# A hybrid decoder layer whose input- and output-projection weights are split once, kept in DRAM as split halves, and reloaded by later chunks

## The chip, the cores and the metric

One core of one Trainium2 chip runs the whole layer. The metric is the device time of one execution in microseconds (us). In what follows PE is the tensor engine, DVE the vector engine, ACT the scalar engine, and SP the engine whose only work here is to issue DMAs, one after the other in the order of its program. All matmuls that matter are float32r matmuls.

## The reference, cut to what matters

```python
h = concat([meta, x])                                  # 16 + 2048 positions, 1024 channels
u = _rmsnorm(h, mix_norm_g)
p = u @ w_in                                           # 1024 x 1792
y = concat([pool_mixer(p_pool), conformer_conv(p_bval, p_bgate), rglru(p_cgate, p_cx)])
h = h + y @ w_out                                      # 1024 x 1024
u = _rmsnorm(h, mlp_norm_g)
h = h + square(relu(u @ w_up)) @ w_down                # 1024 x 4096, 4096 x 1024
out = _rmsnorm(h, final_norm_g)[16:]
```

## The kernel before

Channels lie on the 128 partitions, positions along the row. The 2048 positions are worked in four chunks, c = 0 to 3, of 512 (chunk 0 has the 16 meta positions besides). To keep float32 accuracy at the speed of float32r, every operand is split into a high and a low half: ACT writes `hi` (a copy rounded to float32r) and DVE writes `lo = src - hi` (`split`, L109 to L111), and each product is made as three matmuls, hi·hi, hi·lo, lo·hi.

**Weights.** A block of weights (128 output channels by 1024 inputs) comes as two DMAs of 128x512 float32 (256 KB) into tiles `wr` (6 buffers). Each is split into a tile `wh` of 128x2x512 (hi and lo side by side, 512 KB, 4 buffers). One `wh` tile serves 4 blocks of 128 inputs times three products, 12 matmuls, before its buffer comes free. Class `Weights` (L244) runs down a list of sources: at each item it has splits made up to 4 tiles ahead (`LA_SPLIT`) and DMAs up to 10 tiles ahead (`LA_DMA`).

**Items.** PE's work is a list of items (L923 on): W (a block of the input projection), O (a block of the output projection, 8 to a chunk), U and D (the MLP's up and down projections). The order is W of chunks 0 and 1 together, O of 0, the last four W blocks of chunk 1, then for every chunk U and D, and after D of chunk 0 the eight O items of chunk 1 and the fourteen W items of chunk 2; after D of chunk 1 likewise O of 2 and W of 3; O of 3 stands inside D of 2. "The O stage of chunk c" below means those eight items, 16 weight tiles.

**What else runs in the O stage of chunks 1 and 2.** The finished chunk's output norm is made and stored (`gen_final`, `d_out<-h`). Each O item's result is added on DVE to a piece of the input x, that a DMA brings into a tile `xr` (`evac_o`, L708; 2 `xr` buffers). The next chunk but one's x is loaded through the same two `xr` buffers, squared for its norm on ACT and split into eight `U` tiles (`gen_x`, L404); the W items that follow need all eight. An O item accumulates in a PSUM tile `pm` with 4 buffers, so item j cannot start before item j-4 has been added and its bank freed. Two short matmuls by a matrix of ones (`colsum`, L322, tile `pb`) sum the squares over the channels; a square root on ACT and a RECIPROCAL on DVE follow (`rsqrt_of`).

**Order.** The program text gives each operation a place, but the instruction order on each engine is set by a list scheduler with a model of its own, in which the weight splits have a raised priority (`tc.high_priority(EARLY)`). Every engine, SP too, then executes its list strictly in order: an instruction that waits for a semaphore holds up all behind it.

Of the kernel before, what the change touches and what calls it, by code (L numbers as in the profile page):

```python
# [25 lines left out]
F32 = mybir.dt.float32  # L26
# [4 lines left out]
P = 128  # L31
D = 1024
KB = D // P
# [11 lines left out]
WR = 6  # L45
# [20 lines left out]
for _n, _c in _VECS:  # L66
# [5 lines left out]
_WORDER = (  # L72
    [("bv", 0, 2), ("bg", 0, 4), ("bv", 1, 3), ("bg", 1, 5)]
    + [("cx", i, 10 + i) for i in range(4)]
    + [("ua", i, i) for i in range(2)]
    + [("z", i, 6 + i) for i in range(4)]
)


def build(nc, tc, x0, xr, w_in, w_out, w_fold, w_up, w_down, vecs, gates, pools, pws, out):  # L80
# [10 lines left out]
    dp = es.enter_context(tc.tile_pool(name="dp", bufs=1, space=bass.MemoryType.DRAM))  # L91
# [3 lines left out]
    def nm(s):  # L95
        uid[0] += 1
        return f"{s}_{uid[0]}"

    def t_(tag, cols, bufs, dt=F32):
        shape = [P] + (list(cols) if isinstance(cols, (list, tuple)) else [cols])  # L100
        return sb.tile(shape, dt, name=nm(tag), tag=tag, bufs=bufs)
# [7 lines left out]
    def split(hi, lo, src):  # L109
        A.activation(out=hi, in_=src, func=AF.Copy)  # L110
        V.tensor_tensor(out=lo, in0=src, in1=hi.bitcast(F32), op=ALU.subtract)  # L111
# [21 lines left out]
    cst = {}  # L133

    wo_fold = dp.tile([KB, P, 512], F32, name="wo_fold", tag="wo_fold")
    sums = [dp.tile([P, 2048], F32, name=f"sums_{u}", tag=f"sums_{u}") for u in range(NU)]

    def w_raw(src, tag="xr", bufs=2, queue=nc.sync):
        n = src.shape[-1]
        t = t_(tag, 512, bufs)[:, :n]  # L140
        queue.dma_start(out=t, in_=src)
        return t

    def split_to(hi, lo, raw, scale=None):
        if scale is None:
            split(hi, lo, raw)
        else:
            A.activation(out=hi, in_=raw, func=AF.Copy, scale=scale)
            V.scalar_tensor_tensor(out=lo, in0=raw, scalar=scale, in1=hi.bitcast(F32), op0=ALU.mult, op1=ALU.subtract)
# [6 lines left out]
    def gen_fold():  # L156

        pl, pw = b_tile(), b_tile()
        r1, r2 = w_raw(pools), w_raw(pws)
        split(pl[:, 0, :256], pl[:, 1, :256], r1)  # L160
        split(pw[:, 0, :512], pw[:, 1, :512], r2)
        yield 1300

# [78 lines left out]


    class Weights:  # L244
        def __init__(self, srcs):
            self.srcs = srcs
            self.raw = {}
            self.hl = {}
            self.nd = 0
            self.ns = 0  # L250

        def dma(self, n):
            while self.nd < min(n, len(self.srcs)):
                self.raw[self.nd] = w_raw(self.srcs[self.nd](), "wr", WR, nc.sync if self.nd > 1 else nc.scalar)
                self.nd += 1

        def split(self, n):
            while self.ns < min(n, len(self.srcs)):
                self.dma(self.ns + 1)
                t = t_("wh", (2, 512), WH, F32R)  # L260
                with tc.high_priority(EARLY):
                    split(t[:, 0], t[:, 1], self.raw.pop(self.ns))
                self.hl[self.ns] = t
                self.ns += 1

# [683 lines left out]
    def sources(it):  # L949

        kind, c, j, _ = it
        if kind == "U" and c:
            m1, m2, s = w_up[2 * j], w_up[2 * j + 1], sums[j]
            aps = (
                (m1, 0), (m1, 512), (s, 0), (s, 1536), (s, 1024), (s, 512), (m2, 512),
            )
            return ("U", j), [lambda a=a, c0=c0: a[:, c0 : c0 + 512] for a, c0 in aps]
        if kind == "W":
            a = w_in[_WORDER[j][2]]
        elif kind == "U":  # L960
            a = w_up[j]
        elif kind == "D":
            a = w_down[j // KB, j % KB]
        else:
            return ("O", j), [lambda: wo_fold[j], lambda: w_out[j]]
        return (kind, a.offset if hasattr(a, "offset") else j, j), [lambda a=a, c0=c0: a[:, c0 : c0 + 512] for c0 in (0, 512)]

    srcs, windex, last = [], [], None
    for it in items:
        key, aps = sources(it)  # L970
        if it[0] == "U":
            key = ("U", it[1] > 0, it[2])
        if it[0] == "W":
            key = ("W", _WORDER[it[2]][2])
        if key != last:
            first = len(srcs)
            srcs.extend(aps)
            last = key
        windex.append(first)
    wts = Weights(srcs)  # L980

# [7 lines left out]
    for n, it in enumerate(items):  # L989
# [29 lines left out]
        if kind == "W":  # L1019
            wk, i, _ = _WORDER[j]  # L1020
# [96 lines left out]
def _program():  # L1117
    nc = bacc.Bacc("TRN2", target_bir_lowering=False, num_devices=1, dynamic_dma_scratch_size=1024)
    args = [nc.dram_tensor("d_" + n, list(s), F32, kind="ExternalInput").ap() for n, s in _SHAPES.items()]
    out = nc.dram_tensor("d_out", [NCH, KB, P, NT], F32, kind="ExternalOutput").ap()  # L1120
    with tile.TileContext(nc) as tc:
        build(nc, tc, *args, out)
    return nc
# [8 lines left out]
```

## Time and profile before

| | |
|---|---|
| median of 3 runs | 1967.27 us (1966.43 to 1970.16) |
| the profiled execution | 1964.15 us, of which its span is 1962.2 us |
| PE busy | 1932.9 us, 99% of the span |
| DVE busy | 1508.6 us, 77% |
| ACT busy | 1097.9 us, 56% |
| DMA traffic | 285.07 MB, mean 145 GB/s |

The profile is of one execution. A row of the groups of instructions reads: line, engine, operation, the tile written and the tiles read, the count, then busy time in us and the mean duration of one in ns, and the idle time of the engine just before them with what ended it. In a timeline each row has the start in us, the duration in us, the engine, the line and the tiles; a figure in square brackets is the idle time ahead of it and what released it. "SPq" is SP's queue of DMA issues. A row of the table by stretches has the length of the stretch, the busy time of each engine with its number of instructions, the granted clock of PE as a share of the full one (PEclk), the busy share of the 16 DMA engines, and GB/s.

### The profile page before, as it was taken

The numbers are of one execution on the slowest core, as the hardware profiler recorded it, in microseconds if no ns is written. First come the engines' busy times: TensorE is split into PE (matmuls) and PEld (weight loads), VectorE is DVE, ScalarE is ACT, GpSimd is POOL, SyncE is SP. The second block draws the span as 40 slices with busy tenths as digits, with TensorE's granted clock in tenths as the row PEclk, the third lists the DMA queues.
The fourth block names the chain that finished last, engine by engine and source line by source line (L and its number), as shares of the span: only waits on it lengthen the run. The fifth ranks groups of instructions, "written<-read, shape, count | busy, mean of one in ns | idle before, by whom it ended". The sixth has DMA issues, their size and how long they took to land.

```text
span 1962.2 us, 29710 instructions
## 1 busy us (share of the span) xinstructions
PE 1932.9 (99%) x10648; PEld 1664.7 (85%) x10648; DVE 1508.6 (77%) x2419; ACT 1097.9 (56%) x1837; POOL 0.2 (0%) x4
## 2 busy tenths in 40 slices
PE   8999999999999999999999999999999999999998
PEld 8888878878888789898898778988989889889897
DVE  7986689977756899985776799986768597656477
ACT  6575463646544536675575453775658356445374
POOL 0000000000000000000000000000000000000000
PEclk9999999999999999999999999999999999999999
DMA  6412456645755435353444543544435434545354
GB/s 199 135 44 76 129 169 218 212 159 171 267 174 162 144 92 168 90 166 108 146 133 125 184 127 108 151 115 141 139 117 163 132 103 151 170 137 151 113 173 150
DMA packets 160035, 285.07 MB, mean 145 GB/s; under 512 B 17552, under 2 KB 23824, under 8 KB 159888
## 3 DMA queue, kind: packets, MB, share of 16 engines
q1 hardware_dynamic: 158304, 281.55, 46.6%
q8 instruction: 83, 1.36, 0.3%
q10 hardware_dynamic: 1584, 1.64, 0.2%
q14 instruction: 64, 0.52, 0.1%
HBM read 255.85 MB, written 27.26 MB: 144 GB/s over the span
## 4 chain that ended last, share of the span: by engine, by line
PE 77%; DVE 11%; DMA 6%; issue 3%; ACT 3%; SPq 1%; ACTq 0%; DVEq 0%
PE pm L278 47%; PE pm L302 11%; PE pw L302 9%; PE pm L292 7%; DVE wh L111 3%; DMA s<-d_w_up 2%; DMA xr<-d_xr 2%; DVE ca L535 1%; DMA t<-d_w_up 1%; DVE t L569 1%; DVE fr L821 1%; ACT wh L110 1%; DVE U L795 0%; DMA sums<-s 0%; PE pb L311 0%
## 5 line engine op out<-in xcount | busy, mean ns | idle before, releaser
L110 ACT ACTIVATE wh<-wr 128x512 fp32r<-128x512 f32 x828 | 517.1, 627 | 710.4 <-PE pm L278 482.9
L278 PE MATMUL pm<-U,wh 128*128 128x512 f32 (+1 forms) x3504 | 788.2, 384 | 0.6 <-DVE wh L111 0.6
L278 PEld LDWEIGHTS pm<-U,wh 128*128 128x128 f32 x3504 | 635.2, 188 | 141.0 <-DVE wh L111 1.0
L111 DVE TENSOR_TENSOR wh<-wr,wh 128x512 fp32r<-128x512 f32 x828 | 567.4, 689 | 208.6 <-ACT wh L110 204.1
L278 PE MATMUL pm<-H,wh 128*128 128x512 f32 (+1 forms) x2112 | 450.2, 372 | 8.0 <-ACT wh L110 6.5
L278 PEld LDWEIGHTS pm<-H,wh 128*128 128x128 f32 x2112 | 370.6, 190 | 82.9 <-ACT wh L110 6.5
L302 PE MATMUL pm<-H,wh 128*128 128x256 f32 x2304 | 292.5, 282 | 2.3 <-DVE wh L111 1.4
L302 PEld LDWEIGHTS pm<-H,wh 128*128 128x128 f32 x2304 | 282.3, 188 | 5.2 <-DVE wh L111 2.2
L302 PE MATMUL pw<-H,wh 128*128 128x256 f32 x1728 | 223.2, 282 | 1.6 <-DVE fr L821 1.6
L302 PEld LDWEIGHTS pw<-H,wh 128*128 128x128 f32 x1728 | 212.0, 189 | 4.6 <-DVE fr L821 3.9
L292 PE MATMUL pm<-U,wh 128*128 128x512 f32 (+1 forms) x768 | 176.1, 388 | 0.0
L292 PEld LDWEIGHTS pm<-U,wh 128*128 128x128 f32 x768 | 140.2, 188 | 30.9 <-DVE U L795 0.2
L535 DVE SCALAR_TENSOR_TENSOR ca<-Pbv,vec,ca 128x512 f32<-128x512 f32 x180 | 128.1, 748 | 0.0
L850 DVE TENSOR_TENSOR h<-h,pm 128x512 f32<-128x512 f32 (+1 forms) x106 | 71.6, 675 | 60.5 <-PE pm L278 45.6
L795 DVE TENSOR_TENSOR U<-fr,U 128x512 fp32r<-128x512 f32 x128 | 87.6, 687 | 11.4 <-ACT fr L794 11.4
L793 ACT ACTIVATE U<-fr 128x512 fp32r<-128x512 f32 x128 | 79.6, 624 | 1.9
L794 ACT ACTIVATE fr<-fr 128x512 f32<-128x512 f32 x128 | 79.3, 622 | 1.1
L821 DVE TENSOR_TENSOR fr<-pw,fr 128x512 f32<-128x512 f32 x96 | 66.1, 689 | 4.5 <-PE pw L302 1.9
L346 DVE TENSOR_TENSOR ss<-ss,fr 128x512 f32<-128x512 f32 (+1 forms) x82 | 53.3, 650 | 15.9 <-ACT fr L345 15.3
L337 DVE RECIPROCAL rs<-rs 128x512 f32<-128x512 f32 (+2 forms) x17 | 53.9, 3169 | 10.8 <-ACT rs L335 10.6
L535 DVE SCALAR_TENSOR_TENSOR ca<-h,vec,ca 128x512 f32<-128x512 f32 x60 | 42.8, 748 | 0.1
L841 ACT ACTIVATE fr<-fr 128x512 f32<-128x512 f32 x48 | 30.0, 625 | 12.1 <-DVE fr L840 11.8
(211 smaller groups left out, 1153.0 us busy)
## 6 DMA issues: line engine op xcount, KB each, us to landing
wr<-d_w_down SPq DMA_DIRECT2D x272, 256.0 KB, 2.9
wr<-d_w_up SPq DMA_DIRECT2D x208, 256.0 KB, 2.9
wr<-sums SPq DMA_DIRECT2D x192, 256.0 KB, 3.3
wr<-d_w_in SPq DMA_DIRECT2D x90, 256.0 KB, 2.7
xr<-d_xr SPq DMA_DIRECT2D x56, 256.0 KB, 2.8
wr<-wo_fold SPq DMA_DIRECT2D x32, 256.0 KB, 2.6
wr<-d_w_out SPq DMA_DIRECT2D x32, 256.0 KB, 2.6
s<-d_w_up SPq DMA_DIRECT2D x32, 256.0 KB, 3.8
```

Of the source, the lines that this page charges most:

```text
L110: A.activation(out=hi, in_=src, func=AF.Copy)
L111: V.tensor_tensor(out=lo, in0=src, in1=hi.bitcast(F32), op=ALU.subtract)
L278: T.matmul(ps[:, : s1 - s0], w[k // 4][:, a, (k % 4) * P : (k % 4 + 1) * P], rhs[k][:, b, s0:s1], start=(k == 0 and j == 0), stop=(k == KB ...
L292: T.matmul(ps[:, : s1 - s0], w[k // 4][:, a, (k % 4) * P : (k % 4 + 1) * P], rhs[k][:, b, s0:s1], start=(k == 0 and j == 0), stop=(k == KB ...
L302: T.matmul(ps, w[:, a, k * P : (k + 1) * P], op[k // 2][:, b, (k % 2) * 256 : (k % 2) * 256 + 256], start=(k == 0 and j == 0), stop=(k == ...
L337: V.reciprocal(rs[:, c0:c1], rs[:, c0:c1])
L535: V.scalar_tensor_tensor(out=a, in0=o.ub[i][:, k : k + NT], scalar=vc("cw", i * CONVK + k), in1=a, op0=ALU.mult, op1=ALU.add)
L793: A.activation(out=f[:, 0], in_=r, func=AF.Square)
L794: A.activation(out=r, in_=r, func=AF.Square)
L795: V.tensor_tensor(out=f[:, 1], in0=r, in1=f[:, 0].bitcast(F32), op=ALU.subtract)
L821: V.tensor_tensor(out=out.rearrange("p (a c) -> p a c", a=2), in0=ps.rearrange("p (a c) -> p a c", a=2), in1=x.unsqueeze(1).broadcast_to([ ...
L850: V.tensor_tensor(out=h, in0=h, in1=ps[:, : s1 - s0], op=ALU.add)
```

## The change

When a W or O weight tile is split for the first time, the split tile `wh` (hi and lo) is also stored to DRAM, into `w_kept` or `o_kept`. Each later use of the same block loads the 512 KB from there straight into a `wh` buffer: no `wr` tile, no ACT copy, no DVE subtraction. U and D weights are handled as before. The load is traced where the split was, at the same raised priority, and goes out on SP, as does the store.

```diff
+    w_kept = [[dp.tile([P, 2, 512], F32, name=f"wk_{b}_{q}", tag=f"wk_{b}_{q}") for q in range(2)] for b in range(14)]
+    o_kept = [[dp.tile([P, 2, 512], F32, name=f"ok_{j}_{q}", tag=f"ok_{j}_{q}") for q in range(2)] for j in range(KB)]
...
         def dma(self, n):
             while self.nd < min(n, len(self.srcs)):
-                self.raw[self.nd] = w_raw(self.srcs[self.nd](), "wr", WR, nc.sync if self.nd > 1 else nc.scalar)
+                if self.srcs[self.nd][2] is not None:
+                    self.nd += 1
+                    continue
+                self.raw[self.nd] = w_raw(self.srcs[self.nd][0](), "wr", WR, nc.sync if self.nd > 1 else nc.scalar)
                 self.nd += 1
...
                 t = t_("wh", (2, 512), WH, F32R)
+                _, keep, kept = self.srcs[self.ns]
                 with tc.high_priority(EARLY):
-                    split(t[:, 0], t[:, 1], self.raw.pop(self.ns))
+                    if kept is not None:
+                        nc.sync.dma_start(out=t.bitcast(F32), in_=kept)
+                    else:
+                        split(t[:, 0], t[:, 1], self.raw.pop(self.ns))
+                if keep is not None:
+                    nc.sync.dma_start(out=keep, in_=t.bitcast(F32))
                 self.hl[self.ns] = t
...
+        keep = (None, None)
         if kind == "W":
-            a = w_in[_WORDER[j][2]]
+            b = _WORDER[j][2]
+            if c > 1 or ("W", b) in seen:
+                return [(None, None, t) for t in w_kept[b]]
+            a, keep = w_in[b], w_kept[b]
...
         else:
-            return ("O", j), [lambda: wo_fold[j], lambda: w_out[j]]
+            if c:
+                return [(None, None, t) for t in o_kept[j]]
+            return [(lambda: wo_fold[j], o_kept[j][0], None), (lambda: w_out[j], o_kept[j][1], None)]
+        return [(lambda a=a, c0=c0: a[:, c0 : c0 + 512], keep[c0 // 512], None) for c0 in (0, 512)]
```

Of the 828 `wh` tiles 112 are now loaded whole (64 of W, 48 of O), and 44 are stored (28 and 16). Lines behind the edits move down, by 13 in the region of interest: `xr<-d_xr` of `gen_x` is L412 before and L425 after, that of `evac_o` L713 and L726, `d_out<-h` L873 and L886.

The scheduler orders SP, DVE, ACT and PE anew. Three places matter.

SP, in the O stage of chunk 1, before. The rows begin with the last store of the finished chunk's output (`d_out<-h`). The rows of L412 load the x tiles of chunk 2, from the second on; the row of L713 is the x piece for O item 2; `wr` rows are weights.

```order
L873 DMA d_out<-h_351_2160 128x512
L412 DMA xr_939_5549<-d_xr 128x512
L412 DMA xr_942_5557<-d_xr 128x512
L141 DMA wr_969_5652<-wo_fold_75 128x512
L141 DMA wr_970_5654<-d_w_out 128x512
L141 DMA wr_980_5703<-d_w_in 128x512
L412 DMA xr_945_5565<-d_xr 128x512
L141 DMA wr_981_5705<-d_w_in 128x512
L713 DMA xr_952_5607<-d_xr 128x512
L141 DMA wr_988_5745<-d_w_in 128x512
L412 DMA xr_956_5615<-d_xr 128x512
```

The same place after. `wh<-ok_6_0` is the first half of O item 6, `ok_7` belongs to item 7, `wk_2_0` to the first W item of chunk 2.

```order
L886 DMA d_out<-h_343_2228 128x512
L271 DMA wh_960_5755<-ok_6_0_116 128x1024
L425 DMA xr_919_5583<-d_xr 128x512
L425 DMA xr_922_5591<-d_xr 128x512
L271 DMA wh_961_5757<-ok_6_1_117 128x1024
L271 DMA wh_966_5791<-ok_7_0_118 128x1024
L425 DMA xr_925_5599<-d_xr 128x512
L726 DMA xr_930_5635<-d_xr 128x512
L271 DMA wh_967_5793<-ok_7_1_119 128x1024
L425 DMA xr_934_5643<-d_xr 128x512
L425 DMA xr_937_5651<-d_xr 128x512
L271 DMA wh_972_5827<-wk_2_0_80 128x1024
```

The second and third x tile now stand behind the load of item 6's first half, the fourth and the x piece of item 2 behind item 7's first half, and the fifth and sixth behind item 7's second half; before, raw weight loads stood there. Each `wh` load waits for the last matmul of the tile four places ahead of it in the list of weights, whose buffer it takes.

In the O stage of chunk 2 SP has the same pattern with single rows: the second x tile of chunk 3 stands behind item 6's first half, the third behind its second half, the fourth behind item 7's first half, the x piece of O item 2 and the fifth to eighth tile behind item 7's second half.

DVE, at the end of the O stage of chunk 2, before: the last of chunk 3's eight `U` tiles, the low half for the sum of its squares (`hl`), then the addition that ends O item 3 (`h<-pm,xr`), and two rows on the RECIPROCAL for chunk 3's norm.

```order
L149 SCALAR_TENSOR_TENSOR U_1770_10421<-xr_1771_10422,vec_1_69,U_1770_10421 128x512
L111 TENSOR_TENSOR hl_1781_10471<-ss_1741_10324,hl_1781_10471 128x512
L715 TENSOR_TENSOR h_1779_10466<-pm_1777_10439,xr_1778_10464 128x512
L111 TENSOR_TENSOR wh_1809_10609<-wr_1787_10488,wh_1809_10609 128x512
L337 RECIPROCAL rs_1783_10477<-rs_1783_10477 128x512
```

The same place after.

```order
L151 SCALAR_TENSOR_TENSOR U_1704_10317<-xr_1705_10318,vec_1_69,U_1704_10317 128x512
L111 TENSOR_TENSOR hl_1713_10361<-ss_1677_10226,hl_1713_10361 128x512
L350 RECIPROCAL rs_1715_10367<-rs_1715_10367 128x512
L728 TENSOR_TENSOR h_1711_10356<-pm_1709_10329,xr_1710_10354 128x512
L728 TENSOR_TENSOR h_1720_10401<-pm_1718_10374,xr_1719_10399 128x512
```

The RECIPROCAL has moved ahead of the addition that ends O item 3. In the O stage of chunk 1 the addition still stands ahead of the RECIPROCAL.

SP, at the start of the program, after: behind the loads of x for chunk 0 the first two rows are stores of split tiles, and only then come the next raw weights. Before, the raw weights stood directly behind the loads of x.

```order
L395 DMA t_25_166<-d_x0 128x528
L275 DMA wk_2_0_80<-wh_27_170 128x1024
L275 DMA wk_2_1_81<-wh_28_174 128x1024
L143 DMA wr_36_200<-d_w_in 128x512
L143 DMA wr_38_206<-d_w_in 128x512
```

The two stores wait for the DVE halves of the first two splits, and the raw weights wait behind them. PE's order is that of before but for the places of single `pb` matmuls.

More of the change, by code (lines that the diff above doesn't have):

```diff
@@ L956, in sources @@
             )
-            return ("U", j), [lambda a=a, c0=c0: a[:, c0 : c0 + 512] for a, c0 in aps]
+            return [(lambda a=a, c0=c0: a[:, c0 : c0 + 512], None, None) for a, c0 in aps]
+        keep = (None, None)
         if kind == "W":
-            a = w_in[_WORDER[j][2]]
+            b = _WORDER[j][2]
+            if c > 1 or ("W", b) in seen:
+                return [(None, None, t) for t in w_kept[b]]
+            a, keep = w_in[b], w_kept[b]
         elif kind == "U":
@@ L964, in sources @@
         else:
-            return ("O", j), [lambda: wo_fold[j], lambda: w_out[j]]
-        return (kind, a.offset if hasattr(a, "offset") else j, j), [lambda a=a, c0=c0: a[:, c0 : c0 + 512] for c0 in (0, 512)]
-    srcs, windex, last = [], [], None
-    for it in items:
[L970 to L974, printed above, removed]
+            if c:
+                return [(None, None, t) for t in o_kept[j]]
+            return [(lambda: wo_fold[j], o_kept[j][0], None), (lambda: w_out[j], o_kept[j][1], None)]
+        return [(lambda a=a, c0=c0: a[:, c0 : c0 + 512], keep[c0 // 512], None) for c0 in (0, 512)]
+    srcs, windex, last, seen = [], [], None, set()
+    for it in items:
+        kind, c, j, _ = it
+        key = (kind, j if kind != "W" else _WORDER[j][2])
+        if kind == "U":
+            key += (c > 0,)
         if key != last:
             first = len(srcs)
-            srcs.extend(aps)
+            srcs.extend(sources(it))
             last = key
+            seen.add(key)
         windex.append(first)
```

## Prediction

> **What bounds the kernel now.** The page's first part comes first, then PE's own waits.
>
> ```profile
> PE 1932.9 (99%) x10648; PEld 1664.7 (85%) x10648; DVE 1508.6 (77%) x2419; ACT 1097.9 (56%) x1837; POOL 0.2 (0%) x4
> PE pm L278 <- ACT wh L110: 6.5, 1, 6.5
> PE pb L327 <- ACT hl L110: 4.2, 3, 1.8
> ```
>
> PE is busy nearly throughout; its longest wait for a weight split is the single one before the first matmul. The rows of the two halves of a split and the stretches of the projections follow.
>
> ```profile
> L110 ACT ACTIVATE wh<-wr 128x512 fp32r<-128x512 f32 x828 | 517.1, 627 | 710.4 <-PE pm L278 482.9
> L111 DVE TENSOR_TENSOR wh<-wr,wh 128x512 fp32r<-128x512 f32 x828 | 567.4, 689 | 208.6 <-ACT wh L110 204.1
> 183.00:229.00 46.00, 46.00 (x200) 36.86 (x198) 24.04 (x37) 17.39 (x29) 0.00 (x0) 1.00 0.49 148
> 609.00:660.00 51.00, 47.98 (x198) 37.81 (x198) 40.76 (x55) 26.79 (x44) 0.00 (x0) 0.97 0.59 187
> 660.00:738.00 78.00, 78.00 (x336) 63.02 (x335) 75.06 (x133) 32.86 (x54) 0.00 (x0) 1.00 0.35 107
> 1088.00:1136.00 48.00, 46.68 (x198) 36.31 (x196) 39.48 (x54) 24.23 (x41) 0.00 (x0) 1.00 0.62 198
> 1136.00:1215.00 79.00, 79.00 (x339) 63.44 (x339) 76.01 (x127) 33.61 (x55) 0.00 (x0) 1.00 0.36 107
> ```
>
> The stretches are the O stage of chunk 0, then O of chunk 1, W of 2, O of 2 and W of 3. In both W stages DVE is busy 96% of the time and PE all of it: no split is late there. The only loose stretches are the O stages of chunks 1 and 2, and there PE does not wait for weights. PE's timeline at both places, and SP's:
>
> ```profile
> 608.82 3.18 PE L278 MATMUL pm<-H,wh 128*128 128x512 f32 x13
> 650.42 0.50 PE L327 MATMUL pb<-hl,ones 128*128 128x512 f32 x1 [1.83 <-ACT hl L110]
> 652.60 7.12 PE L278 MATMUL pm<-H,wh 128*128 128x512 f32 x24 [0.53 <-DVE h L715]
> 1087.90 3.18 PE L278 MATMUL pm<-H,wh 128*128 128x512 f32 x13
> 1129.59 0.50 PE L328 MATMUL pb<-hl,ones 128*128 128x512 f32 x1 [0.23 <-DVE hl L111]
> 1130.19 5.85 PE L278 MATMUL pm<-H,wh 128*128 128x512 f32 x24
> 628.32 1.00 SPq L412 DMA_DIRECT2D xr<-d_xr  x2
> 633.15 0.33 SPq L412 DMA_DIRECT2D xr<-d_xr  x1
> 635.02 0.33 SPq L713 DMA_DIRECT2D xr<-d_xr  x1
> 1105.52 1.04 SPq L412 DMA_DIRECT2D xr<-d_xr  x2
> ```
>
> O of chunk 1 begins at 608.82. Seven of its eight items run without a break, 7 × 5.6 us at the rate worked out below and two short sums, to about 648.5; the last starts at 652.60, 43.8 us in, after waits for the norm's sum and for `h L715`, the addition that frees its PSUM bank. In chunk 2 the break is from about 1128 to 1130.19, 42.3 in. What PE waits for is the chain of x loads through two `xr` buffers: from the second x tile on (628.32, 19.5 in; 1105.52, 17.6 in) each load needs a buffer that ACT and DVE have just emptied.
>
> **The change, part by part.** *Removed.* 112 splits: 112 × 0.627 = 70 us of ACT and 112 × 0.689 = 77 us of DVE. Where they go, PE does not wait for them, so I count nothing; at most the waits of the two O stages and single waits in the U stages shrink.
>
> *The loads.* The nearest rows for 512 KB are the loads and stores of 256 KB.
>
> ```profile
> wr<-d_w_out SPq DMA_DIRECT2D x32, 256.0 KB, 2.6
> xr<-d_xr SPq DMA_DIRECT2D x56, 256.0 KB, 2.8
> sums<-s SPq DMA_DIRECT2D x32, 256.0 KB, 3.9
> 1144.77 70.47 PE pm L278 x302
> 490.00:540.00 50.00, 50.00 (x217) 40.52 (x217) 38.59 (x63) 25.38 (x43) 0.00 (x0) 1.00 0.80 266
> ```
>
> A matmul takes 70.47/302 = 0.233 us of PE, a weight tile of 12 takes 2.8. A `wh` load goes out when the tile four ahead is done and has three tiles, 8.4 us, to land. It takes between 2.6 and twice that, 5.2, so it is hidden; I count nothing. Bandwidth: in W, 28 × 0.262 MB more in 78 us is 94 GB/s on top of 107. In O of chunk 0, 16 stores of 0.524 MB in 46 us are 182 on top of 148, 330 GB/s, where the row of 266 at a busy share of 0.80 makes the ceiling 333. The stores have over 8 us of slack; 0 to 4 us, I take 1.
>
> *The start.* The raw weights move behind two stores.
>
> ```profile
> 6.14 8.70 SPq L141 DMA_DIRECT2D wr<-d_w_in  x9
> 7.75 0.69 DVE L111 TENSOR_TENSOR wh<-wr,wh 128x512 fp32r<-128x512 f32 x1 [0.62 <-ACT wh L110]
> 11.38 1.20 ACT L110 ACTIVATE wh<-wr 128x512 fp32r<-128x512 f32 x2
> 23.27 6.02 PE L278 MATMUL pm<-H,wh 128*128 128x264 f32 x47
> ```
>
> The third weight goes out after 8.44 instead of at 6.14, so its split moves from 11.4 to about 14 or 15; PE gets to it in earnest at 23.27. Nothing counted, -1 to +2.
>
> *SP's list in the O stages: the term that matters.* A `wh` load now waits on SP for PE. Queued behind it are the x tiles and the x pieces of the O items, and for those wait ACT, DVE and in the end PE. Before, the raw load of a tile waited for the split six tiles ahead of it in the list, and that for PE to be done four tiles further ahead; now it waits for PE four tiles ahead. What stands behind a weight load of the same number is held about six tiles, 17 us, longer, unless the list was changed to suit.
>
> ```profile
> SPq L141 <- DVE wh L111: 1276.6, 741, 10.1
> 631.09 0.63 ACT L345 ACTIVATE fr<-xr 128x512 f32<-128x512 f32 x1 [1.29 <-DMA xr<-d_xr]
> 632.37 0.75 DVE L149 SCALAR_TENSOR_TENSOR U<-xr,vec,U 128x512 fp32r<-128x512 f32 x1
> 634.24 0.75 DVE L149 SCALAR_TENSOR_TENSOR U<-xr,vec,U 128x512 fp32r<-128x512 f32 x1
> 651.86 0.69 DVE L715 TENSOR_TENSOR h<-pm,xr 128x512 f32<-128x512 f32 x1 [0.34 <-DMA xr<-d_xr]
> 1128.84 0.69 DVE L111 TENSOR_TENSOR hl<-ss,hl 128x512 fp32r<-128x512 f32 x1
> 1130.85 3.35 DVE L337 RECIPROCAL rs<-rs 128x512 f32<-128x512 f32 x1
> ```
>
> From landing (631.09) to a free buffer (632.37 + 0.75) an x tile takes 2.0 us, the second of a pair 1.9 more; a load 2.8 from issue to landing; 0.4 is added for the `wh` load's own issue. Times from the stage's start, x tiles counted from 1:
>
> Chunk 1. Tiles 2 and 3 stand behind item 6's first half, which waits for 9 weight tiles, 25.2: tile 2 goes out at 25.6, lands 28.4, is used 30.4; tile 3 used 32.3. Tile 4 stands behind item 7's first half (11 tiles, 30.8): out 31.2, landed 34.0, used 36.0. Item 2's x piece needs tile 3's buffer: out 32.3, landed 35.1, added 35.8. Item 6 needs that bank and starts at 35.8 instead of 33.6. Tile 5: out 36.0, used 40.8; tile 6 used 42.7; tile 7: out 40.9, used 45.7. Item 3's piece takes its buffer: out 45.8, landed 48.6, added 49.3, and item 7 starts at 49.3, where before it was 43.8: **+5.5 us**.
>
> Chunk 2. Tile 2 used 30.4; tile 3 behind 10 weight tiles, out 28.4, used 33.2; tile 4 behind 11, used 36.0; item 2's piece behind 12, out 34.0, added 37.5, so item 6 starts 3.9 late. Tile 5 used 40.9, tile 6 42.8, tile 7 45.8, tile 8 out 42.9, used 47.7. Now the RECIPROCAL stands ahead of item 3's addition on DVE: `hl` done 48.4; from there to the end of the RECIPROCAL is 1134.20 - 1129.53 = 4.7 by the rows, 53.1; added 53.8, where before it was 42.3: **+11.5 us**.
>
> The landings of all DMAs into `xr`, and the stretches at the breaks of before (the third figure from the end is the clock):
>
> ```profile
> DMA to landing us min/median/max: 2.0/2.8/4.5
> 652.00:656.00 4.00, 3.47 (x10) 2.73 (x10) 3.72 (x2) 1.32 (x2) 0.00 (x0) 0.57 0.60 191
> 1127.00:1131.00 4.00, 2.70 (x10) 1.43 (x9) 3.70 (x7) 3.05 (x6) 0.00 (x0) 1.00 0.63 197
> ```
>
> Bounds: were SP to reach these rows as early as before, both terms are zero or a little below; with the five loads in series at the longest landing, 4.5 us, each is 8.5 more. I take the median, 2.8.
>
> *The clock.* After the break of about 4 us in chunk 1, with two lone matmuls in it, PE ran 4 us at 0.57 of its clock, a loss of 4 × 0.43 = 1.7 us; after the shorter one of chunk 2 it did not. Of the breaks ahead (2.2 and 7.8 in chunk 1, 3.9 and 10.7 in chunk 2) two are new and near 4 or longer: 2 × 1.7 = **+3.4**. The Trainium skill ("TensorE: Matmul & The Clock Gate", Part 1) says that PE falls to half its clock after an idle window of about 3.4 us on a free-running counter and gets it back after a busy window; the trace agrees on the two breaks above. By that rule the break of 3.9 may miss a whole window, and this term would be an estimated 1.7 instead of 3.4, the sum 1.7 less.
>
> *Sum.* 5.5 + 11.5 + 3.4 + 1 = 21.4 us. The profiled execution took 1964.15 (span 1962.2), which makes 1985.6. The median of the runs lies 3.1 above that execution; on its footing the sum is 1988.7, and I say 1988.
>
> **The rivals.** *Freed engines shorten the chain (faster).* Without some 16 splits per O stage on ACT and DVE each x tile is used sooner. If SP still reaches the second x tile by 19.5 us into the stage of chunk 1 (17.6 in chunk 2), the breaks there close: 652.60 - 648.5 = 4.1 and 1.7 of clock in chunk 1, 2.2 in chunk 2, 8.0 in all: 1967.3 - 8.0 = 1959.3. Against it: the `wh` load ahead of that row waits for PE's ninth tile at 25.2, and nothing on ACT or DVE changes that. Chance 0.10.
>
> *Hidden anyway (no change).* PE's 99% absorb it: the x chain is late but PSUM's four banks cover it, gains and losses cancel, 1967. The banks cover four items, and the sum has used them. That the change doesn't do what it says, and the splits stay, can be left out: DVE's list is 113 rows shorter. Chance 0.08.
>
> *The loads themselves are late (slower still).* They decide once a 512 KB load takes over 8.4 us. At 10 us a buffer turns over in 10 + 2.8, with four buffers 3.2 a tile instead of 2.8, and 112 × 0.4 = 45 us make 2033 with the sum. The busy shares of 0.35 in the W stages speak against it. Chance 0.06.
>
> **How the numbers follow.** The forecast, slower through SP's list in the O stages, has 0.76: 1988. A measurement of this kernel can tell about 0.2%, 4 us, from no change. Slower is 0.76 + 0.06 = 0.82, same 0.08, faster 0.10. The range runs from no change, 1967, which leaves out the faster case, to both chains at their long landings, 1988 + 17 = 2005, which leaves out the late loads: 0.84 inside.
>
> **What would show it.** Right: SP waits at L271 for PE's matmuls; the second x tile of the stage goes out some 25 us in instead of 19.5 and 17.6; the last O item starts near 49 and 54 us in; PE waits there for `h L728`; PEclk is under 1 behind both breaks; DVE has about 112 TENSOR_TENSOR rows fewer and the W stages are no shorter. Wrong: the O stages keep their length, or PE waits at L291 for a `wh` DMA in the W stages, or the time is under 1967.

## The result, and the profile after

| | before | after |
|---|---|---|
| median of the runs | 1966.85 us (1965.01 to 1970.16) | 1991.93 us (1991.12 to 1994.62) |
| the profiled execution (its span) | 1964.15 us (1962.2) | 1991.43 us (1989.6) |

The ratio is 1.0128, 95% interval 1.011 to 1.0146: 25 us slower, 4 more than forecast and inside the range. The engines and the split rows of the page after:

```profile
PE 1939.9 (98%) x10648; PEld 1670.5 (84%) x10648; DVE 1441.0 (72%) x2307; ACT 1029.7 (52%) x1724; POOL 0.2 (0%) x4
L110 ACT ACTIVATE wh<-wr 128x512 fp32r<-128x512 f32 x716 | 447.1, 627 | 630.6 <-PE pm L291 405.9
L111 DVE TENSOR_TENSOR wh<-wr,wh 128x512 fp32r<-128x512 f32 x716 | 490.2, 688 | 201.9 <-ACT wh L110 197.9
```

The 112 splits are gone: ACT is busy 68 us less and DVE 68 us less, and the kernel is slower all the same. What PE waits for now (total, times, longest):

```profile
PE pm L291 <- DVE h L728: 15.0, 3, 5.8
PE pb L340 <- ACT hl L110: 9.3, 3, 6.4
PE pm L291 <- ACT wh L110: 6.3, 1, 6.3
PE pb L324 <- ACT hl L150: 4.1, 1, 4.1
```

The first two rows are new in size: the addition that frees a PSUM bank in O, and the sum of squares of the next x. No row of the whole list has a `wh` DMA as the releaser: the kept loads themselves are in time. PE's timeline after, at the O stages of chunks 1 and 2; each stage runs from its first `pm<-H` row to the first `pm<-U` row behind it:

```profile
612.31 3.18 PE L291 MATMUL pm<-H,wh 128*128 128x512 f32 x13
...
650.99 8.12 PE L291 MATMUL pm<-H,wh 128*128 128x512 f32 x24 [4.42 <-DVE h L728]
...
665.51 0.79 PE L340 MATMUL pb<-hl,ones 128*128 128x512 f32 x1 [6.41 <-ACT hl L110]
666.12 1.22 PE L291 MATMUL pm<-H,wh 128*128 128x512 f32 x2
...
673.65 2.72 PE L291 MATMUL pm<-U,wh 128*128 128x512 f32 x11
...
1101.24 3.18 PE L291 MATMUL pm<-H,wh 128*128 128x512 f32 x13
...
1141.19 7.16 PE L291 MATMUL pm<-H,wh 128*128 128x512 f32 x24 [5.84 <-DVE h L728]
...
1157.14 7.68 PE L291 MATMUL pm<-H,wh 128*128 128x512 f32 x24 [4.71 <-DVE h L728]
...
1164.66 3.20 PE L291 MATMUL pm<-U,wh 128*128 128x512 f32 x13
```

The ends of the same stages before:

```profile
659.56 2.72 PE L278 MATMUL pm<-U,wh 128*128 128x512 f32 x11
...
1136.00 6.32 PE L278 MATMUL pm<-U,wh 128*128 128x512 f32 x26
```

These starts, set against 608.82 and 1087.90 before, give the whole account of the span. Up to O of chunk 1: +3.5 us (612.31 - 608.82). That stage: 61.3 us instead of 50.7, **+10.6**. From there to O of chunk 2, with all of W, U and D of a chunk: 427.6 instead of 428.3, -0.7. That stage: 63.4 instead of 48.1, **+15.3**. The rest: -1.3. The sum is the 27.4 by which the span grew. SP's rows after, at the second x tile of each stage, and its longest new wait:

```profile
638.67 0.85 SPq L425 DMA_DIRECT2D xr<-d_xr  x2
...
1127.48 0.38 SPq L425 DMA_DIRECT2D xr<-d_xr  x1
SPq L271 <- PE pm L291: 223.6, 102, 6.1
```

The second x tile goes out 26.4 and 26.2 us into the stage, where before it was 19.5 and 17.6, and the row below it says why: SP stands at L271, the load of a kept split, until PE has emptied a `wh` buffer. The stretches at PE's breaks after (PEclk is the third figure from the end):

```profile
62.00:69.00 7.00, 6.17 (x15) 4.89 (x16) 4.25 (x9) 1.93 (x3) 0.00 (x0) 0.51 0.46 152
649.00:656.00 7.00, 5.01 (x12) 3.96 (x13) 4.43 (x7) 3.56 (x6) 0.00 (x0) 0.51 0.46 158
663.00:670.00 7.00, 4.49 (x11) 3.38 (x12) 5.05 (x7) 3.82 (x6) 0.00 (x0) 0.53 0.40 115
1137.00:1144.00 7.00, 2.81 (x7) 2.26 (x8) 4.24 (x7) 3.11 (x5) 0.00 (x0) 0.52 0.57 186
1151.00:1161.00 10.00, 5.29 (x11) 3.58 (x12) 7.64 (x8) 2.31 (x4) 0.00 (x0) 0.50 0.31 109
```

Each of these stretches of 7 to 10 us ran at half clock. It sets in before the break is over: in the row at 1137 PE is busy for only 2.81 of the 7 us, and it resumes at 1141.19.

### The profile page after: what moved, and what is told of

Same layout as the page of the kernel before. It is cut to its first block, busy times and chain, and to the rows that moved or that the text cites. A ratio compares the mean times of both kernels' runs of the same rounds, so it can differ in the third digit from the quotient of the medians.

```text
span 1989.6 us, 29411 instructions
## 1 busy us (share of the span) xinstructions
PE 1939.9 (98%) x10648; PEld 1670.5 (84%) x10648; DVE 1441.0 (72%) x2307; ACT 1029.7 (52%) x1724; POOL 0.2 (0%) x4
## 4 chain that ended last, share of the span: by engine, by line
PE 87%; DVE 5%; DMA 3%; ACT 3%; issue 2%; SPq 0%; ACTq 0%; DVEq 0%
PE pm L291 56%; PE pm L315 11%; PE pw L315 9%; PE pm L305 9%; DMA xr<-d_xr 2%; DVE wh L111 2%; PE pb L324 1%; ACT wh L110 1%; DVE fr L834 1%; PE pb L325 0%; PE pb L326 0%; DVE t L582 0%; PE pb L413 0%; DMA wr<-d_w_in 0%; DVE U L151 0%
## 5 line engine op out<-in xcount | busy, mean ns | idle before, releaser
L110 ACT ACTIVATE wh<-wr 128x512 fp32r<-128x512 f32 x716 | 447.1, 627 | 630.6 <-PE pm L291 405.9
L111 DVE TENSOR_TENSOR wh<-wr,wh 128x512 fp32r<-128x512 f32 x716 | 490.2, 688 | 201.9 <-ACT wh L110 197.9
L807 ACT ACTIVATE fr<-fr 128x512 f32<-128x512 f32 x128 | 79.1, 621 | 1.0
L358 ACT ACTIVATE fr<-h 128x512 f32<-128x512 f32 (+1 forms) x45 | 27.9, 622 | 67.8 <-DVE h L728 46.1
L548 DVE SCALAR_TENSOR_TENSOR ca<-h,vec,ca 128x512 f32<-128x512 f32 x60 | 42.3, 745 | 0.2 <-ACT ca L545 0.2
```

What stands on the lines that cost most here:

```text
L548: V.scalar_tensor_tensor(out=a, in0=o.ub[i][:, k : k + NT], scalar=vc("cw", i * CONVK + k), in1=a, op0=ALU.mult, op1=ALU.add)
L807: A.activation(out=r, in_=r, func=AF.Square)
```

## The experiments

The theory: the loss is SP's list in the O stages of chunks 1 and 2, where x loads stand behind loads that wait for PE. The rivals: the doubled bytes, and the stores. Each kernel ran beside the kernel before on one chip; the ratio is to that.

**e1, the x loads early in the list.** Only the priority of the two kinds of x load is raised in the changed kernel:

```diff
-            nc.sync.dma_start(out=raw, in_=xr[o.c - 1, k])
+            with tc.high_priority(2 * EARLY):
+                nc.sync.dma_start(out=raw, in_=xr[o.c - 1, k])
```

and the same in `evac_o`.

> The DMAs that load x tiles and x pieces get a higher priority than the loads of the kept weights; queue, waits and bytes are those of the changed kernel, only SP's list differs: the second x tile now stands behind item 4's first half instead of item 6's. Theory 'list' (x loads stand behind weight loads that wait for PE): the second x tile goes out 18 to 21 us into the O stages of chunks 1 and 2 instead of 26, the breaks ahead of the last two O items shrink to a few us, and the time falls from 1992 to 1966 to 1976; the 6 us lost at the start stay. Theory 'traffic' (52 MB more for the DMA engines make loads land late): nothing changes, 1988 to 1996.

1969.78 us, ratio 1.0019 (1.001 to 1.0029): some 21 of the 25 us are gone, with the same queue, loads and bytes. SP's row for the second x tile, and PE's last break in that stage, which begins at 609.92 here:

```profile
626.33 0.99 SPq L426 DMA_DIRECT2D xr<-d_xr  x2
```

```profile
652.90 0.70 PE L340 MATMUL pb<-hl,ones 128*128 128x512 f32 x1 [3.64 <-ACT hl L110]
```

The tile goes out 16.4 us in, earlier than the 18 to 21 that I expected. No wait for the addition (L730 in this kernel) is left in that stage, and one break of 3.6 us at the column sum remains. The stage takes 51.3 us, where it was 61.3 with the change and 50.7 before. In chunk 2 (52.9 us instead of 63.4) DVE's order changed as well: the addition of item 3 (1134.09) stands ahead of the RECIPROCAL (1135.20) again, so there e1 does not show SP's list alone.

**e8, the control.** The same early place in the kernel before, nothing kept.

> The kernel before with the early place for the x loads and nothing kept: the control for e1. If the early place is worth nothing by itself: 1964 to 1968, and e1 shows what the change costs without its list effect, some 3 us. If it gains by itself (the breaks of 1.8 us at the column sum in O go, 1959 to 1963), then e1 hides a cost of 7 to 10 us behind that gain.

1967.21 us, ratio 1.0001 (0.9992 to 1.0011): the early place gains nothing by itself. So e1 undoes most of the harm of the change and adds no gain of its own, and some 3.5 us of the change's cost stay in e1 (1.0019 against 1.0001).

**e5, only the output projection kept.**

```diff
-            a, keep = w_in[b], w_kept[b]
+            a = w_in[b]
```

The two lines that load `w_kept` go too.

> Only the 16 splits of the output projection are stored and loaded again; the input projection's 28 pieces are split for every chunk as before. Theory (SP's list in the O stages of chunks 1 and 2: x tiles and x pieces stand behind loads of kept splits that wait for PE): nearly all of the O-stage loss of 26.0 us stays, without the 6.5 us at the start, where the input projection is stored: 1983 to 1993, with breaks of 4 to 6 us ahead of the last two items of O in chunks 1 and 2. Rival (the loss comes from the input projection's kept loads or stores): 1966 to 1972, breaks of at most 2 us in those two stages.

1988.39 us, ratio 1.0105 (1.009 to 1.012). The breaks stand at the same places (the stage begins at 611.71), and SP's second x tile is as late, 26.3 us in:

```profile
650.19 7.29 PE L290 MATMUL pm<-H,wh 128*128 128x512 f32 x24 [4.24 <-DVE h L727]
663.15 0.80 PE L339 MATMUL pb<-hl,ones 128*128 128x512 f32 x1 [5.68 <-ACT hl L110]
```

```profile
638.03 0.86 SPq L424 DMA_DIRECT2D xr<-d_xr  x2
```

Most of the loss hangs on these 48 loads out of 112, with their 16 stores. In chunk 2 the addition of item 3 stands ahead of the RECIPROCAL here, and the stage takes 58.6 us instead of the 63.4 of the changed kernel; in chunk 1, where the addition stands first in both, it takes 61.4, as there.

**e6, only the input projection kept.** The counterpart: `o_kept` and its loads and stores are gone.

> Only the 28 splits of the input projection are stored and loaded again. Theory (list in the O stages, from the output projection's loads): the start's 6.5 us stay and little else, less some 3 us that the freed engines gave back in the W stages: 1966 to 1973, breaks in the O stages of chunks 1 and 2 of at most 3 us. Rival (the kept loads of the input projection that are issued late in the O stage hold the x pieces as well): 1980 or more, with breaks ahead of the last items of O.

1970.89 us, ratio 1.0015 (1.0006 to 1.0024). The second x tile is out 19.5 us in (the stage begins at 611.28), as before, but the last item still waits:

```profile
630.77 1.00 SPq L424 DMA_DIRECT2D xr<-d_xr  x2
```

```profile
656.65 7.60 PE L290 MATMUL pm<-H,wh 128*128 128x512 f32 x24 [2.90 <-DVE h L727]
```

In chunk 2 that wait is 4.7 us, over the 3 that I expected. It is not SP's list that makes it: DVE has the RECIPROCAL (1133.11, 3.35 us) ahead of item 3's addition (1136.38), as in the changed kernel. In chunk 1 the addition waits for an x piece that goes out at 651.24 and is used at 655.90. Together e5 and e6 account for the change within the intervals: 0.0105 + 0.0015 against 0.0128.

**e2, the kept loads and stores on GpSimd's queue.** SP then has no load of a kept split in its list.

```diff
-                        nc.sync.dma_start(out=t.bitcast(F32), in_=kept)
+                        nc.gpsimd.dma_start(out=t.bitcast(F32), in_=kept)
```

and the store likewise.

> Stores and loads of the kept weights are issued from GpSimd's queue, which has nothing else to do, so that SP's list holds no wait for PE. Theory 'list': the O stages are as long as in the kernel before or shorter, the break at the start (58 us) is gone too, PE has no wait for x pieces over 2 us; 1958 to 1970. Theory 'traffic': the bytes are the same, 1988 to 1996.

1988.67 us, ratio 1.0111 (1.0093 to 1.0128): a miss for the theory, and inside the range of the rival, the traffic. The breaks are still there, at the column sum only. PE's waits, then SP's loads from the second x tile on and ACT's next rows in the O stage of chunk 1, which begins at 618.74:

```profile
PE pb L340 <- ACT hl L110: 18.3, 4, 8.9
```

```profile
636.60 9.77 SPq L425 DMA_DIRECT2D xr<-d_xr  x3
```

```profile
643.99 0.63 ACT L358 ACTIVATE fr<-xr 128x512 f32<-128x512 f32 x1 [8.21 <-DMA xr<-d_xr]
...
647.24 0.63 ACT L358 ACTIVATE fr<-xr 128x512 f32<-128x512 f32 x1 [2.01 <-DMA xr<-d_xr]
```

The second x tile goes out 17.9 us in, which is earlier than the 19.5 of the kernel before, so its place in SP's list is not what makes it late. What is late is the landing: the second and third tile went out together, right behind all eight output stores, and landed 7 and 10 us later, one behind the other, while the core moved 308 to 416 GB/s (635 to 645 us). From there the chain of two buffers ran until 664. So SP's list is not the only way to this loss: with the same bytes bunched ahead of the x loads, the same chain is late through the landings. In the changed kernel the list is the larger part, since e1 moves the same bytes on the same queue. How much of the landings here is the stores' bytes and how much the other queue's was not separated.

**e4, only the stores on GpSimd's queue.**

> Only the stores leave SP, the loads stay there. Theory 'list': the break at 58 us (SP at stores that wait for splits, the folding's weights behind them) goes, and the O stages keep theirs: 1983 to 1989. Theory 'traffic': as the changed kernel, 1989 to 1995.

1997.79 us, ratio 1.0159 (1.0144 to 1.0174): above both expected ranges, and if anything slower than the change itself. The break near 57 us stays, so it isn't SP standing at the stores:

```profile
PE pb L324 <- ACT hl L150: 5.3, 1, 5.3
```

**e3, the bytes without the list.** The kernel before, which makes all its splits, with the 44 stores and 112 loads of 256 KB into a tile that nothing reads, on GpSimd's queue.

> The kernel before (all weights split anew each time), with the bytes of the change added on GpSimd's queue: 44 stores of 512 KB of split tiles, and for each of the 112 later uses a load of 256 KB into a tile that nobody reads, so that each use moves 512 KB as in the changed kernel. Theory 'list': as the kernel before, 1963 to 1973. Theory 'traffic': most of the loss, 1982 to 1995.

2017.02 us, ratio 1.0256 (1.0241 to 1.0271): above both expected ranges and the dearest kernel of all, but not where the question was. In O of chunk 1 the break is that of the kernel before:

```profile
698.52 0.50 PE L336 MATMUL pb<-hl,ones 128*128 128x512 f32 x1 [1.66 <-ACT hl L110]
```

and its losses lie elsewhere, most of them near 57 and 247 us, where on GpSimd's queue each store stands behind a load that waits for the one buffer of the load before. Its loads of the O stages ran ahead of time, so it says nothing on bytes inside them. That is what the next one was for.

**e7, e1 with half the bytes.** Each kept load fetches the high parts alone, and the low parts are cleared; the products with them are left out of the result.

```diff
-                        nc.sync.dma_start(out=t.bitcast(F32), in_=kept)
+                        nc.sync.dma_start(out=t[:, 0].bitcast(F32), in_=kept[:, 0])
+                        nc.gpsimd.memset(t[:, 1].bitcast(F32), 0.0)
```

> As e1 (x loads early in the list), but each of the 112 kept loads fetches only the high parts, 256 KB instead of 512 KB, and GpSimd clears the low parts, so the products with the low parts of the projections are left out of the result from the second use on. Theory with traffic (what is left of the loss in e1, breaks of 3.8 and 4.6 us at the column sum of the O stages, comes from the doubled bytes, which stretch each x piece's load from 2.8 to 3.5 us in a chain of two buffers): those breaks fall to the 1.8 us of the kernel before, x loads land in 2.8 to 3.1 us, 1962 to 1967. Rival (what is left is the order alone): breaks of 3.8 to 4.6 us stay, 1968.5 to 1971.

1963.23 us, ratio 0.9977 (0.9965 to 0.9988), by the ratios 8 us below e1. The break is down, and x loads land in 2.9 us instead of 3.5:

```profile
649.23 0.50 PE L341 MATMUL pb<-hl,ones 128*128 128x512 f32 x1 [2.40 <-ACT hl L110]
```

```profile
xr<-d_xr SPq DMA_DIRECT2D x56, 256.0 KB, 2.9
```

The loads are not only fewer bytes here but also smaller pieces; e9 below takes the two apart. A second reading is against e8, which has the same early place and loads the same 256 KB a tile but makes its splits (and has no stores): e7 is 4 us faster, and the intervals do not overlap. So where the bytes are not doubled, the splits saved are worth a little.

**e9, e1 with each kept load in two of 256 KB.** The bytes are the same, the pieces smaller.

> As e1, but each of the 112 kept loads is issued as two loads of 256 KB, high and low parts, so the bytes are the same and nothing is left out. Theory (size: an x load of 256 KB that stands behind one 512 KB load on SP's queue waits for it, 3.5 us instead of 2.8): x loads land in 2.8 to 3.1 us, the breaks at the column sums of O fall to 2.5 us or less, 1963 to 1966.5. Rival (bytes: whatever the pieces, twice the bytes stretch the x loads): x loads 3.4 us or more, breaks of 3.8 to 4.6 us stay, 1968 to 1972.

1966.12 us, ratio 0.9999 (0.9989 to 1.0009). The time fell into the theory's range, the things it was to fall by did not:

```profile
PE pb L341 <- ACT hl L110: 7.8, 3, 3.9
```

```profile
xr<-d_xr SPq DMA_DIRECT2D x56, 256.0 KB, 3.4
```

x loads take 3.4 us and the longest break 3.9, as the rival had them. I leave the size of the pieces undecided. But e7 and e9 have pieces of one size, and there half the bytes take the ratio from 0.9999 to 0.9977, 4 us, x loads from 3.4 to 2.9 us and the longest break from 3.9 to 2.4. So the bytes are a second, smaller cause: they stretch each link of the x chain.

**e10, e1 with three `xr` buffers, and e11, the kernel before with three.** The one further edit is `t_("xr", NT, 3)` for `t_("xr", NT, 2)` wherever it stands (and the like default in `w_raw`, whose weights use the same buffers).

> As e1, with three buffers instead of two for the x tiles and x pieces (2 KB more per partition). Theory (the x loads form a chain of two buffers, so each load's landing time counts in the O stage): the breaks of 3.8 and 4.6 us at the column sums of O fall below 1.5 us, 1960 to 1965. Rival (the breaks come from the engines behind the loads, the additions on DVE): they stay, 1968 to 1971.

> The kernel before with three buffers for the x tiles and x pieces, nothing kept: the control for e10. Theory: its breaks of 1.8 us at the column sums of O go, 1962 to 1966. If it goes below e10, the change still costs what its bytes and stores cost once the x loads have room; if e10 is lower, the change gains the difference.

1958.10 us, ratio 0.9957 (0.9942 to 0.9972), and 1958.69 us, ratio 0.9961 (0.9946 to 0.9975), both below the ranges that I expected. The stage's column sum in e10, and how long x loads take:

```profile
642.72 0.50 PE L340 MATMUL pb<-hl,ones 128*128 128x512 f32 x1 [0.96 <-ACT hl L110]
```

```profile
xr<-d_xr SPq DMA_DIRECT2D x56, 256.0 KB, 3.8
```

and in e11:

```profile
641.73 0.50 PE L327 MATMUL pb<-hl,ones 128*128 128x512 f32 x1 [1.30 <-ACT hl L110]
```

An x load takes longer in e10 than in e1, 3.8 us, and PE hardly waits: with a third buffer the landing time hardly counts. Both beat the kernel before by 8 us, and they are equal within the intervals: with room for x and the early place, keeping the splits neither costs nor gains on the whole. The O stage of chunk 1 takes 47.2 us in both. The equality is a balance, though: e10 reaches that stage 4.1 us later (611.00 against 606.95) and makes it up behind it. The kernel before with both the third buffer and the early place was not run, so this is not yet a like-for-like pair.

**e12, the third buffer alone on the changed kernel.**

> The changed kernel with the third buffer alone, and no early place for the x loads. Where the changed kernel's list has one x load before its run of waiting loads and seven more loads of kept splits ahead of the next x loads, this one has two, and the next ones stand where they stood. Theory (the place in SP's list): the third x load still leaves 24 to 27 us into the O stages of chunks 1 and 2, so of the O stages' 26 us only a part goes: 1970 to 1982. Rival (the depth of the buffers is the whole cause, as e10 and e11 would also allow): as e10, 1956 to 1962.

1967.18 us, ratio 1.0003 (0.9992 to 1.0013): below my 1970 and well above the rival's 1962. SP's third x load and PE's break (the stage begins at 609.39):

```profile
635.73 0.38 SPq L425 DMA_DIRECT2D xr<-d_xr  x1
```

```profile
653.79 0.79 PE L340 MATMUL pb<-hl,ones 128*128 128x512 f32 x1 [4.20 <-ACT hl L110]
```

The load stands where the theory put it, 26.3 us in, but two x tiles are in by then and what is left goes through three buffers: 25 us come back for one buffer, and the early place is worth 9 more (e10). Against e11, which differs by the change alone, e12 is 8 us slower (1.0003 against 0.9961), so three buffers without the early place do not make the change free. I read the place in the list and the depth of the buffers as one cause seen from two sides: either shortens the chain of x loads.

## Why the prediction was right, point by point

*What bounds it, and the splits counted at nothing.* Nearly right. DVE has 112 rows fewer, as forecast, and from W of chunk 2 to O of chunk 2 the kernel gained 0.7 us in 428 although 136 us of work left ACT and DVE over the kernel. It is not quite nothing, as the 4 us between e8 and e7 show.

*The kept loads hidden.* Right for PE: no wait for them in the list of waits. What the step left out is that their bytes slow other loads: e7 with half of them is 4 us below e9.

*Bandwidth in O of chunk 0, +1.* Not to be seen. PE's busy time between 150 and 600 us, with that stage inside, is up:

```profile
150.00:600.00 450.00, 447.84 (x1928) 360.86 (x1926) 339.14 (x527) 242.26 (x394) 0.00 (x0) 1.00 0.55 174
```

```profile
150.00:600.00 450.00, 449.71 (x1937) 363.24 (x1936) 338.18 (x523) 245.94 (x398) 0.00 (x0) 1.00 0.60 199
```

The first row is before, the second after: 1.9 us gained. The ceiling of 333 GB/s was too low besides: e2 moved up to 416 GB/s.

*The start, nothing counted.* Wrong: a break of 4.1 us and 7 us at half clock (6.17 us of PE's busy time, so some 3 lost) stand there, of which +3.5 is left by 612 us. The step looked at the raw weights behind the first two stores. What came late is the folding weight that `hl L150` needs. It comes through the same two `xr` buffers, behind the x tiles of chunk 1: the last of these goes out at 45.6 instead of 38.5, the first folding weight at 57.9 instead of 50.5. From 20 to 62 us the DMA engines are busy 81% instead of 48%, and x loads land in 4.0 us instead of 3.0. It is not SP waiting at the stores (e4); e6, which keeps only W, has a 3.1 us break there, e5, which keeps only O, 1.7, and e1, with the same stores, 0.4, with its first matmul 4 us later instead. Whether the list or the stores' traffic makes it was not separated.

*SP's list.* Right in place and kind, too small. Forecast: second x tile near 25 us in, last items at 49.3 and 53.8. Measured: 26.4 and 26.2; the last items start 53.8 us in (666.12 - 612.31) and 55.9 (1157.14 - 1101.24). Against 43.8 and 42.3 before, the chains cost 10.0 and 13.6 us, 23.6 in all, where the sum had 17.0. In chunk 2 the RECIPROCAL does stand ahead of item 3's addition:

```profile
1153.18 3.35 DVE L350 RECIPROCAL rs<-rs 128x512 f32<-128x512 f32 x1 [1.60 <-ACT rs L348]
1156.45 1.22 DVE L728 TENSOR_TENSOR h<-pm,xr 128x512 f32<-128x512 f32 x2
```

The mis-sized part is, in the main, one landing. Item 6 starts 38.7 and 40.0 us in instead of 35.8 and 37.5, and the second x tile, for which ACT waits there in both stages, accounts for it:

```profile
638.24 0.33 SPq L271 DMA_DIRECT2D wh<-ok  x1
```

```profile
643.59 0.63 ACT L358 ACTIVATE fr<-xr 128x512 f32<-128x512 f32 x1 [14.22 <-DMA xr<-d_xr]
...
1132.79 0.63 ACT L358 ACTIVATE fr<-xr 128x512 f32<-128x512 f32 x1 [16.04 <-DMA xr<-d_xr]
```

It was issued 0.4 us behind a 512 KB load (638.67 against 638.24) and used 4.9 us after its own issue (643.59 - 638.67), 5.3 in chunk 2 (1132.79 - 1127.48), where I took the median of all x loads, 2.8. That is 2.1 and 2.5 too little; the bound of the range, 4.5, was too low as well. That the bytes are behind it is what e7 against e9 speaks for, where half of them made x loads and breaks shorter; on this one load it was not tested. The 1.6 us more of item 7 in chunk 1 come in the main from a load that the sum left out. Tile 7's buffer is free at 655.67, when DVE ends its row for tile 5, but on SP the first load of a W split stands ahead of tile 7's, and it waits for the first half of item 6, which PE works through at half clock:

```profile
656.34 0.33 SPq L271 DMA_DIRECT2D wh<-wk  x1
656.77 0.37 SPq L425 DMA_DIRECT2D xr<-d_xr  x1
```

That is 1.1 us, and a landing of 3.5 us (used at 660.30) where the sum had 2.8 adds 0.7. PE's row there names the column sum (`hl L110`), which stands just ahead of item 7, and not `h L728` as forecast; but the addition ends at the same time (it starts at 665.38 and takes 0.68 us, item 7 starts at 666.12). The RECIPROCAL in chunk 2 was sized right: 4.7 in the sum, a wait of 4.71 behind it, and a stage 4.9 us shorter in e5, which doesn't have it there.

*The clock, +3.4.* Two breaks were counted, and four were followed by half clock. But what is lost ahead of a wait for x is next to no loss, so only the part behind the last items counts: 10.6 - 10.0 and 15.3 - 13.6, 2.3 us. The rule of the Trainium skill that I weighed ("TensorE: Matmul & The Clock Gate", Part 1), from which I took that a break of 3.9 us may miss a window, stays untried, since that break came out at 5.8.

*The sum.* 23.6 + 2.3 in the O stages instead of 20.4, +3.5 up to there instead of 1, and 2.0 given back elsewhere: 27.4 instead of 21.4. Of the rivals, the freed engines (1959) and no change (1967) fell with SP's rows, the late loads (2033) with PE's waits.

## What to carry to other kernels

When a load replaces work, ask what the new load waits for and what stands behind it on the engine that issues it: here a load that waited for PE took the place of one that waited for a split further back, and loads of quite other data paid. Look for the shortest chain of buffers that passes through that queue; one more buffer there gave 25 us back to the changed kernel and 8 to the old one. Compare the other engines' lists too: the RECIPROCAL that the scheduler put ahead of an addition cost another 4.7 us. And price the work that is removed on the path that ends last, not by its busy time: 136 us of ACT and DVE were worth a few us at most.

## What the runs showed of the hardware

The half clock came in spells of 7 and 10 us at breaks of 4 to 6 us, each beginning before PE was back at its items, where the prediction had 4 us behind one break; in e10, whose breaks in the O stages are under 2 us, there is none:

```profile
641.00:648.00 7.00, 6.04 (x27) 4.49 (x26) 5.35 (x6) 3.36 (x6) 0.00 (x0) 1.00 0.78 266
1113.00:1120.00 7.00, 5.41 (x23) 4.15 (x23) 5.66 (x5) 2.21 (x4) 0.00 (x0) 1.00 0.87 260
```

The Trainium skill ("TensorE: Matmul & The Clock Gate", Part 1) has the clock come back after one busy window of about 3.4 us. The spells here are about two and three of these long, with PE busy for 2.8 to 6.2 us of them.

DMAs issued by GpSimd were dearer than SP's: 0.54 us of the issuing engine against 0.33, and the 512 KB stores of W landed in 4.5 us (e4) instead of 3.5.
